# A bundle of schedule and buffer changes in a two-layer convolution and sparse-attention trunk on one core

## The chip, the core and the metric

One core of a Trainium2 chip. TensorE (PE) multiplies matrices, VectorE (DVE), ScalarE (ACT) and GpSimd (POOL) work on tiles in on-chip memory (SBUF) and, POOL excepted here, on the matrix results in PSUM; SyncE (SP) issues most DMAs. Each engine works through its own instructions in order and waits on semaphores for the others. The metric is the device time of one execution in microseconds (us).

## What is computed

Two layers over 1024 tokens of width 1024. Layer A is a gated convolution over time with a memory cross-attention beside it; layer B is a sparse attention, in which an indexer picks 256 keys a token, with its own memory attention.

```python
for i in range(DEPTH):                       # 2: layer A, layer B
    if i % N_MIXERS == 0:
        u, qm, gate = split_cols(x @ a_w_in[j], A_SIZES)
        y_mix = conformer_conv(u, ...)       # a*sigmoid(g), 31 taps a channel (1536 channels), LayerNorm, SiLU
    else:
        q, k, v, qi, ki, wi, qm, gate = split_cols(x @ b_w_in[j], B_SIZES)
        y_mix = dsa_attention(...)           # 8 index heads: sum of w*relu(qi.ki); top 256; 12 heads, one key head
    y_mem = mem_cross_attention(qm, mem_n, w_mkv)   # 4 heads into 256 memory tokens, softmax
    y = jnp.concatenate([y_mix, y_mem], axis=-1) * jax.nn.silu(gate)
    x = layer_norm(ALPHA * x + y @ w_out, pg, pb)
```

## The kernel before

Channels lie on the partitions and tokens on the free axis: a block of 128 output channels of a projection is 8 k-tiles x 3 products x 2 token halves = 48 matmuls of 128x128 by 512 columns. The three products are those of a value split in a high and a low part (`xhi`, `xlo`; weights `wh`, `wl`): high by high, low by high, high by low (L149 to L153). ACT makes a weight's high part (`wh`), POOL its low part (`wl`); activations are split from PSUM by ACT (high) and DVE (low, L169), in SBUF by ACT and POOL. Projection results stand in PSUM banks (`pj`, a ring); transposes and other small results in `pt`.

**Start and layer A.** The eight x tiles (`xn`) are transposed by `x_in` into a two-bank PSUM tile of the tag `acc` and split. `u_pair` projects a pair of channel blocks in two halves of 512 tokens, then `conv_pair` runs the 31 taps: ACT writes the scaled input to a PSUM tile `acc` (two of them), 30 taps on DVE (L429) add to it, the last one writes the SBUF tile `co`. `conv_stat` subtracts a channel mean `c_sh`, taken from the first block by a matmul with ones into an `acc` tile (`cmean`), and sums for the LayerNorm. Between the projections stand the four memory heads (`head_a`): memory tokens are transposed (`mt` to `pt` to `mf` to `mhi`, `mlo`), keys and values projected, scores, softmax (`mem_scores`: DVE maximum, ACT exponential with its sum, DVE reciprocal, POOL product by it), transposes, values. `k_b` and `v_b` do layer B's keys and values into one tile `kvr` of the tag `mp`, of which there is one buffer and which the softmax uses too. Gates are `silu_gate` (`ga`, `msgA`).

**Layer B.** Projections of gates and queries are fill, work that depends only on the layer's input. In the index stage PE makes scores `S` per index head, ACT takes the `relu`, DVE adds the weighted heads to `xs`; after each head PE issues `FILL` matmuls of gate projection. In the threshold stage DVE and ACT search the 256th largest score per token (`threshold`, `select`), while PE projects the remaining gates (`gates[FREE_GATES:]`, results through SiLU to DRAM) and the queries of the first `EARLY_Q` = 2 heads (`head_q`, high part on ACT L823, low part on DVE L824). In the attention, for each head and pair of token blocks, PE makes `S`, a DVE operation masks it and takes the maximum, ACT exponentiates, POOL divides (L975), PE transposes (`pt`), ACT and DVE split, PE multiplies by the values (`pv`). After each transposed pair `between` issues `share` steps of a fill: the query of the next head, so four blocks in three heads and one memory head; the last gate (`LATE_GATES`) is the end of it. Each query so made stays in SBUF. Output groups (L599 to L601) follow.

The order of each engine's instructions is set by a scheduler with priorities (`low`, `issue_after`) and by the tile pools, whose rings make a writer wait until the last reader is done.

## Time and profile before

| | |
|---|---|
| median of 3 runs | 1702.32 us (1701.68 to 1703.47) |
| the profiled execution | 1699.66 us |
| its span | 1697.8 us |
| PE busy | 1647.7 us, 97% |
| DVE busy | 1148.6 us, 68% |
| ACT busy | 748.3 us, 44% |
| POOL busy | 668.7 us, 39% |

Stages, in us from the span's start: layer A to about 560, its output and layer B's inputs to 860, index 860 to 914, threshold 914 to 1088, attention 1082 to about 1525, output groups to the end, with the output of the memory heads among them. A row of the time line has the start, the length, engine, line, operation and in brackets the idle time before it and what ended that.

### The profile page before, as it was taken

To read this page: it belongs to the slowest core of one execution; us is meant where nothing else is said; L and a number is where in the kernel's file an instruction comes from. 1 tells how busy PE (TensorE), PEld (TensorE's weight loads), DVE (VectorE), ACT (ScalarE), POOL (GpSimd) and SP (SyncE) were. 2 spreads that over 40 slices of the span, in tenths; PEclk is the share of its full clock that TensorE was granted. 3 is DMA by queue.
4 is the path that set the end of the run, shared out by engine and by line. 5 is a ranking of instruction groups with operands and counts; after the bars stand their busy time and mean duration, and the time that the engine had idled before them with its cause. 6 is when DMAs were issued, how large, how long until landed. Compare 5 with 4: busy or idle time off the path is not lost.

```text
span 1697.8 us, 22413 instructions
## 1 busy us (share of the span) xinstructions
PE 1647.7 (97%) x8214; PEld 1380.4 (81%) x8214; DVE 1148.6 (68%) x1798; ACT 748.3 (44%) x1395; POOL 668.7 (39%) x577
## 2 busy tenths in 40 slices
PE   8999999999989999999989999899999999999997
PEld 6877888888878788888867877688888889888886
DVE  3799999989997565256168999765455555535337
ACT  4333344444343542124466776154454544533221
POOL 2344554635556366234322332133232323332233
PEclk9999999999999999999999999899999999999999
DMA  5121212222234553122311323212122121246212
GB/s 190 46 58 66 87 51 87 63 75 63 87 124 148 206 167 131 47 79 103 84 44 51 97 83 99 82 50 69 51 75 63 61 64 50 69 163 235 87 44 99
DMA packets 137789, 152.69 MB, mean 90 GB/s; under 512 B 7946, under 2 KB 108298, under 8 KB 137680
## 3 DMA queue, kind: packets, MB, share of 16 engines
q1 hardware_dynamic: 137680, 151.27, 27.9%
q8 instruction: 64, 1.05, 0.3%
q14 instruction: 45, 0.37, 0.1%
HBM read 112.71 MB, written 36.70 MB: 88 GB/s over the span
## 4 chain that ended last, share of the span: by engine, by line
PE 52%; DVE 12%; ACT 3%; issue 2%; DMA 1%; POOL 1%; DVEq 0%; ACTq 0%; SPq 0%; POOLq 0%
PE pj L149 7%; PE pj L151 7%; PE pj L153 7%; PE pj L601 5%; PE pj L600 5%; PE pj L599 5%; DVE junk L846 4%; PE pt L995 2%; DVE xs L805 2%; PE pt L600 2%; PE pt L599 2%; PE pt L601 2%; PE S L965 1%; PE S L967 1%; PE S L966 1%
## 5 line engine op out<-in xcount | busy, mean ns | idle before, releaser
L149 PE MATMUL pj<-xhi,wh 128*128 128x512 f32 (+2 forms) x1328 | 523.4, 394 | 13.8 <-DVE ql L824 7.2
L153 PE MATMUL pj<-xhi,wl 128*128 128x512 f32 (+2 forms) x1328 | 521.6, 393 | 0.0
L151 PE MATMUL pj<-xlo,wh 128*128 128x512 f32 (+2 forms) x1328 | 520.7, 392 | 0.2 <-DVE xlo L169 0.2
L132 POOL TENSOR_TENSOR wl<-wr,wh 128x512 fp32r<-128x512 f32 x258 | 340.4, 1326 | 437.9 <-ACT wh L131 420.1
L429 DVE SCALAR_TENSOR_TENSOR acc<-h,chan,acc 128x996 f32<-128x996 f32 (+27 forms) x348 | 418.5, 1263 | 16.1 <-ACT acc L419 14.7
L149 PEld LDWEIGHTS pj<-xhi,wh 128*128 128x128 f32 (+1 forms) x1328 | 250.7, 189 | 67.3 <-DVE ql L824 7.4
L153 PEld LDWEIGHTS pj<-xhi,wl 128*128 128x128 f32 (+1 forms) x1328 | 250.6, 189 | 49.8 <-issue 0.5
L151 PEld LDWEIGHTS pj<-xlo,wh 128*128 128x128 f32 (+1 forms) x1328 | 250.8, 189 | 48.6 <-DVE xlo L169 1.0
L131 ACT ACTIVATE wh<-wr 128x512 fp32r<-128x512 f32 (+1 forms) x230 | 143.8, 629 | 317.5 <-PE pj L151 162.7
L975 POOL TENSOR_SCALAR t<-t,smB 128x128 f32<-128x128 f32 (+3 forms) x96 | 72.0, 751 | 183.5 <-DVE smB L974 95.3
L600 PE MATMUL pj<-wl,xhi 128*128 128x512 f32 x320 | 124.1, 390 | 0.0
L599 PE MATMUL pj<-wh,xhi 128*128 128x512 f32 x320 | 123.5, 391 | 0.4 <-ACT xhi L559 0.3
L601 PE MATMUL pj<-wh,xlo 128*128 128x512 f32 x320 | 122.6, 390 | 0.0
L970 DVE CUSTOM_DVE_ANT_0 t<-S,xs 128x128 f32<-128x128 f32 (+3 forms) x96 | 70.9, 755 | 74.2 <-PE S L967 49.9
L169 DVE TENSOR_TENSOR pl<-pt,ph 128x512 fp32r<-128x512 f32 (+1 forms) x120 | 69.2, 580 | 59.4 <-ACT ph L168 58.5
L168 ACT ACTIVATE ph<-pt 128x512 fp32r<-128x512 f32 (+1 forms) x120 | 60.3, 509 | 77.5 <-PE pt L995 70.6
L973 ACT ACTIVATE t<-t,mxB 128x128 f32<-128x128 f32 (+3 forms) x96 | 74.1, 774 | 45.4 <-DVE mxB L972 45.3
L852 ACT ACTIVATE junka<-xs,cand 128x896 bf16<-128x896 f32 (+2 forms) x93 | 80.3, 864 | 29.3 <-DVE cand L877 23.0
L846 DVE TENSOR_SCALAR_CACHE_REDUCE junk<-xs,cand 128x1024 bf16<-128x1024 f32 (+2 forms) x93 | 89.9, 967 | 2.2
L599 PEld LDWEIGHTS pj<-wh,xhi 128*128 128x128 f32 x320 | 60.1, 188 | 14.0 <-ACT xhi L559 1.2
L601 PEld LDWEIGHTS pj<-wh,xlo 128*128 128x128 f32 x320 | 60.0, 188 | 13.0
L600 PEld LDWEIGHTS pj<-wl,xhi 128*128 128x128 f32 x320 | 60.1, 188 | 12.9
(296 smaller groups left out, 2792.9 us busy)
## 6 DMA issues: line engine op xcount, KB each, us to landing
wr<-in_a_w_in_dram SPq DMA_DIRECT2D x88, 256.0 KB
wr<-in_b_w_in_dram SPq DMA_DIRECT2D x76, 256.0 KB
wr<-in_a_w_out_dram SPq DMA_DIRECT2D x32, 256.0 KB
wr<-in_b_w_out_dram SPq DMA_DIRECT2D x32, 256.0 KB
yraw<-yb SPq DMA_DIRECT2D x16, 512.0 KB
gb<-gB SPq DMA_DIRECT2D x15, 512.0 KB
yb<-yB SPq DMA_DIRECT2D x12, 512.0 KB
sgB<-gb SPq DMA_DIRECT2D x11, 512.0 KB
```

What stands on the lines that cost most here:

```text
L131: nc.scalar.activation(hi, raw, AF.Copy)
L132: nc.gpsimd.tensor_tensor(lo, raw, hi.bitcast(F32), op=OP.subtract)
L149: nc.tensor.matmul(o, wh, xh, start=(k == 0), stop=False)
L151: nc.tensor.matmul(o, wh, xl, start=False, stop=False)
L153: nc.tensor.matmul(o, wl, xh, start=False, stop=(k == KD - 1))
L429: nc.vector.scalar_tensor_tensor(dst[:, s:], h[:, :T - s], w, acc[:, s:], op0=OP.mult, op1=OP.add)
L599: nc.tensor.matmul(o, yh[:, k, tsl], wh, start=(k == 0), stop=False)
L600: nc.tensor.matmul(o, yh[:, k, tsl], wl, start=False, stop=False)
L601: nc.tensor.matmul(o, yl[:, k, tsl], wh, start=False, stop=(k == 3))
L846: nc.vector.tensor_scalar(j[:, :nk(b)], xs(b), th[:, i:i + 1], None, op0=op, op1=OP.add, accum_out=c[:, i:i + 1])
L852: nc.scalar.activation(j[:, :nk(b)], xs(b), AF.Sign, bias=th[:, i:i + 1], scale=-(2.0 ** 24), accum_out=c[:, i:i + 1])
L973: nc.scalar.activation(t, t, AF.Exp, bias=mx[:, e:e + 1], scale=s, accum_out=sm[:, e:e + 1])
```

## The change

1. **Start.** `wake` transposes the identity nine times before x is there. Tiles 2, 3 and 6 are transposed by halves in single banks; tiles 4 to 7 behind the first half projection and not ahead of the second; the rows of the layer's parameters are loaded and transposed at the second pair.
2. **Taps.** ACT writes the scaled input to `co` in SBUF. The first tap (s = 1) reads it and writes `acc`, the last (s = 2) writes `co`; column 1 is finished by an operation of one column.
3. **Mean.** The two halves of `cmean` go to two `pt` banks; a copy to `sumd` goes.
4. **Memory heads of layer A.** ACT multiplies by the reciprocal; the tag `mp` has two buffers, layer B's keys one of their own (`kr`), and are stored apart from the values.
5. **Layer B.** Two gates are fill in the index stage, two matmuls per head. Two late gates. Three queries (`SPILL`) are projected in the threshold stage and stored to DRAM as they are, the others and the late gates in the attention as one stream; each is fetched again by a DMA, split by ACT and POOL. The early queries' low part is made by POOL from a copy by ACT. The fill per transposed pair stays at 4 (memory heads 8).

```diff
-AHEAD = 1
-SHARE = (4, 8, 4)
-FREE_GATES = 1
+SHARE = (4, 8)
+FREE_GATES = 2
+SPILL = 3
-FILL = {7: 1, 6: 1, 5: 1, 4: 1, 3: 1, 2: 1}
-LATE_GATES = (11,)
+FILL = {7: 2, 6: 2, 5: 2, 4: 2, 3: 2, 2: 2}
+LATE_GATES = (10, 11)
...
+        def transpose_halves(src, t, bank):
+            for g in range(2):
+                o = bank()
+                for k in range(4):
+                    c = slice((4 * g + k) * P, (4 * g + k + 1) * P)
+                    nc.tensor.transpose(o[:, k * P:(k + 1) * P], src[:, c], ident)
+                split_ps(xhi[:, 4 * g:4 * g + 4, t * P:(t + 1) * P], xlo[:, 4 * g:4 * g + 4, t * P:(t + 1) * P],
+                         o.rearrange("p (a b) -> p a b", a=4))
...
+                if tags["p"][2] == 2:
+                    nc.scalar.activation(pn[:, i, :], pn[:, i, :], AF.Copy, scale=sm[:, i:i + 1])
+                else:
+                    nc.gpsimd.tensor_scalar(pn[:, i, :], pn[:, i, :], sm[:, i:i + 1], 1.0, op0=OP.mult, op1=OP.mult)
...
-                if start and hf == 1:
+                og = psum()
+                project(pg, xhi, xlo, hf * 512, 512, og)
+                if start and hf == 0:
                     for t in range(4, NB):
                         x_in(t)
+                if i == 1 and hf == 0:
                     rows_in()
-                og = psum()
-                project(pg, xhi, xlo, hf * 512, 512, og)
...
+            pair = (i0, i0 + 1)
+            accs = [psb.tile([P, T], F32, tag="acc", bufs=2, name=f"acc{i}") for i in pair]
+            for i, h in zip(pair, hs):
+                conv_out[i] = co_tile(f"co{i}")
+                nc.scalar.activation(conv_out[i], h, AF.Identity, bias=chan[:, i, TAPS:TAPS + 1],
+                                     scale=chan[:, i, TAPS - 1:TAPS])
+
+            for s in (1, *range(TAPS - 1, 1, -1)):
+                for i, h, acc in zip(pair, hs, accs):
                     w = chan[:, i, TAPS - 1 - s:TAPS - s]
+                    src, dst = (conv_out[i] if s == 1 else acc), (conv_out[i] if s == 2 else acc)
+                    nc.vector.scalar_tensor_tensor(dst[:, s:], h[:, :T - s], w, src[:, s:], op0=OP.mult, op1=OP.add)
+                    if s == 1:
+                        nc.vector.scalar_tensor_tensor(src[:, 1:2], h[:, 0:1], w, src[:, 1:2], op0=OP.mult, op1=OP.add)
...
-                o = psb.tile([P, T], F32, tag="acc", bufs=2, name="cmean")
                 for hf in range(2):
                     hs = slice(hf * 512, (hf + 1) * 512)
-                    nc.tensor.matmul(o[:, hs], ones, d[:, hs], start=True, stop=True)
-                    nc.scalar.activation(c_sh[:, hs], o[:, hs], AF.Copy, scale=1.0 / P)
+                    o = psum_t()
+                    nc.tensor.matmul(o, ones, d[:, hs], start=True, stop=True)
+                    nc.scalar.activation(c_sh[:, hs], o, AF.Copy, scale=1.0 / P)
...
+            raw = am.tile([P, NMEM], F32, tag="kr", bufs=1, name=f"kr{h}")
+            mem_k(b_w_mkv, h, raw=raw)
+            nc.sync.dma_start(kvb_dram[h][:, :NMEM], raw)
...
+                if early:
+                    raw = bq.tile([P, 512], F32, tag="qr", bufs=1, name=f"qr{h}_{hf}")
+                    nc.scalar.activation(raw, o, AF.Copy, scale=c)
+                    nc.gpsimd.tensor_tensor(ql[:, hs], raw, qh[:, hs].bitcast(F32), op=OP.subtract)
+                    continue
...
+        def raw_steps(c0, dst, pc, scale=1.0):
+            for hf in range(2):
+                o = psum()
+                yield from project_steps(pc, xhi, xlo, hf * 512, 512, o)
+                raw = bq.tile([P, 512], F32, tag="qr", bufs=1, name=f"qr{uid()}")
+                nc.scalar.activation(raw, o, AF.Copy, scale=scale)
+                nc.sync.dma_start(dst[:, hf * 512:(hf + 1) * 512], raw)
...
+        def fetch(h):
+            qh = bq.tile([P, T], F32R, tag="qh", bufs=2, name=f"qh{h}")
+            ql = bq.tile([P, T], F32R, tag="ql", bufs=2, name=f"ql{h}")
+            raw = ql.bitcast(F32)
+            nc.sync.dma_start(raw, q_d[h])
+            nc.scalar.activation(qh, raw, AF.Copy)
+            nc.gpsimd.tensor_tensor(ql, raw, qh.bitcast(F32), op=OP.subtract)
...
+            for h in line[EARLY_Q:EARLY_Q + SPILL]:
+                run(spill(h, POOL_W))
             for h in range(EARLY_Q):
-                run(head_q(h, load_cols(b_w_in, h * P)))
+                run(head_q(h, load_cols(b_w_in, h * P), True))
...
+                todo = [spill(h) for h in line[EARLY_Q + SPILL:]] + [late_gate(i) for i in LATE_GATES]
```

The new order at three places. PE at the channel mean before, `pj` 1059 being the second half of the first gate, `mt` the memory tokens:

```order
L153 MATMUL pj_1059<-xhi,wl_1030 128x512
L440 MATMUL cmean<-co_583,ones 128x512
L285 MATMUL pt_1010<-ident,mt_954 128x128
L285 MATMUL pt_1010<-ident,mt_967 128x128
L285 MATMUL pt_1000<-ident,mt_954 128x128
L285 MATMUL pt_1000<-ident,mt_967 128x128
L440 MATMUL cmean<-co_583,ones 128x512
L285 MATMUL pt_1010<-ident,mt_954 128x128
L285 MATMUL pt_1010<-ident,mt_967 128x128
L149 MATMUL pj_1111<-xhi,wh_1089 128x512
```

PE there after, followed by fourteen more transposes of `mt` and then by `pj` 1130:

```order
L153 MATMUL pj_1078<-xhi,wl_1049 128x512
L464 MATMUL pt_608<-co_542,ones 128x512
L464 MATMUL pt_611<-co_542,ones 128x512
L304 MATMUL pt_999<-ident,mt_973 128x128
L304 MATMUL pt_999<-ident,mt_986 128x128
```

ACT there after, up to the SiLU that frees the two banks of the first gate:

```order
L305 ACTIVATE mf_1010<-pt_1009,chan 128x256
L172 ACTIVATE mhi<-mf_1000 128x512
L172 ACTIVATE mhi<-mf_1010 128x512
L468 ACTIVATE sumsq<-co_542 128x1024
L305 ACTIVATE mf_1020<-pt_1019,chan 128x256 x2
L305 ACTIVATE mf_1030<-pt_1029,chan 128x256
L172 ACTIVATE mhi<-mf_1020 128x512
L340 ACT_TABLE_LOAD
L340 ACTIVATE ga_1039<-pj_1052 128x512
L340 ACTIVATE ga_1039<-pj_1078 128x512
```

The transposes of the memory tokens, which stood between projections, now stand together behind the mean.

PE in the index stage before (`S`: scores of one index head, `pj`: the gate that is fill):

```order
L149 MATMUL pj_6913<-xhi,wh_6902 128x512
L794 MATMUL S_6918<-khh,qs_6656 128x512
L795 MATMUL S_6918<-kll,qs_6656 128x512
L794 MATMUL S_6918<-khh,qs_6656 128x512
L795 MATMUL S_6918<-kll,qs_6656 128x512
L151 MATMUL pj_6913<-xlo,wh_6902 128x512
```

and after:

```order
L149 MATMUL pj_6940<-xhi,wh_6929 128x512
L151 MATMUL pj_6940<-xlo,wh_6929 128x512
L818 MATMUL S_6946<-khh,qs_6683 128x512
L819 MATMUL S_6946<-kll,qs_6683 128x512
L818 MATMUL S_6946<-khh,qs_6683 128x512
L819 MATMUL S_6946<-kll,qs_6683 128x512
L153 MATMUL pj_6940<-xhi,wl_6930 128x512
L149 MATMUL pj_6940<-xhi,wh_6929 128x512
```

Two matmuls of fill stand where one stood.

DVE at the end of the selection before (`ql`: low parts of the first query; `t`: the first masked scores):

```order
L824 SCALAR_TENSOR_TENSOR ql_8988<-pj_8989,qh_8987 128x512
L917 SCALAR_TENSOR_TENSOR eq_8033<-cs_8034,room_8038,eq_8033 128x896
L919 SCALAR_TENSOR_TENSOR xs_6309<-eq_8033,xs_6309 128x896
L824 SCALAR_TENSOR_TENSOR ql_8988<-pj_9016,qh_8987 128x512
L970 ISA t_0_9144,mxB_0_9138<-S_9140,xs_6307 128x128
```

and after:

```order
L977 SCALAR_TENSOR_TENSOR room_8145<-less_8139,cs_8141 128x1
L978 SCALAR_TENSOR_TENSOR eq_8140<-cs_8141,room_8145,eq_8140 128x896
L980 SCALAR_TENSOR_TENSOR xs_6336<-eq_8140,xs_6336 128x896
L1033 ISA t_0_9345,mxB_0_9339<-S_9341,xs_6334 128x128
```

The low parts of the queries are no longer between the selection and the first scores.

## Rows read from the trace of the kernel before

**Rows 1.** The page, part 1: engine, busy us, share of the span, instructions.

```profile
PE 1647.7 (97%) x8214; PEld 1380.4 (81%) x8214; DVE 1148.6 (68%) x1798; ACT 748.3 (44%) x1395; POOL 668.7 (39%) x577
```

**Rows 2.** Waits of PE, whole span: us in total, times, longest us.

```profile
PE pj L149 <- DVE ql L824: 7.2, 1, 7.2
PE S L794 <- ACT relu L800: 5.9, 7, 1.7
PE pj L149 <- ACT ga L321: 4.7, 2, 3.4
...
PE pj L149 <- ACT kvr L298: 1.3, 1, 1.3
```

**Rows 3.** Windows: stretch, its us, PE busy (count), other engines; an output group.

```profile
1524.00:1628.00 104.00, 104.00 (x459) 86.02 (x459) 43.37 (x54) 27.64 (x36) 32.88 (x23) 1.00 0.44 157
```

**Rows 4.** Time line of PE, between the first two half projections.

```profile
29.63 0.93 PE L263 MATMUL pj<-ident,rows 36*128 36x36 f32 x12
31.09 1.09 PE L242 MATMUL px<-ident,xn 128*128 128x128 f32 x8 [0.53 <-DVE xlo L169]
33.30 1.04 PE L149 MATMUL pj<-xhi,wh 128*128 128x512 f32 x2 [1.11 <-ACT xhi L168]
```

**Rows 5.** Time line of PE at the channel mean.

```profile
123.65 1.02 PE L440 MATMUL cmean<-co,ones 128*128 128x512 f32 x2
124.52 0.94 PE L285 MATMUL pt<-ident,mt 128*128 128x128 f32 x4
125.51 1.12 PE L440 MATMUL cmean<-co,ones 128*128 128x512 f32 x2
129.04 0.66 PE L285 MATMUL pt<-ident,mt 128*128 128x128 f32 x2 [2.41 <-ACT co L428]
131.01 0.79 PE L149 MATMUL pj<-xhi,wh 128*128 128x512 f32 x1 [1.31 <-ACT ga L321]
...
136.14 0.40 PE L149 MATMUL pj<-xhi,wh 128*128 128x512 f32 x1
```

**Rows 6.** Time line of ACT in the same stretch.

```profile
121.78 0.57 ACT L286 ACTIVATE mf<-pt,chan 128x256 f32<-128x256 f32 x1 [0.50 <-PE pt L285]
122.37 0.63 ACT L172 ACTIVATE mhi<-mf 128x512 fp32r<-128x512 f32 x1
...
129.07 1.28 ACT L321 ACT_TABLE_LOAD   x1
```

**Rows 7.** Time lines of ACT and DVE in layer A's fourth memory head.

```profile
489.17 0.20 ACT L355 ACTIVATION_READ_ACCUMULATOR mp<-pt,mx 128x1 f32 x1
...
497.54 0.39 ACT L298 ACTIVATE kvr<-pj 128x256 f32<-128x256 f32 x1
...
490.79 0.17 DVE L357 RECIPROCAL sm<-sm 128x4 f32<-128x4 f32 x1
```

**Rows 8.** The index stage: window row, and a row of DVE's time line.

```profile
860.00:914.00 54.00, 47.75 (x204) 33.59 (x203) 44.00 (x48) 39.09 (x53) 8.52 (x11) 1.00 0.09 23
...
868.47 6.83 DVE L805 SCALAR_TENSOR_TENSOR xs<-relu,win,xs 128x1024 f32<-128x1024 f32 x5
```

**Rows 9.** Time lines of PE and DVE where the attention begins.

```profile
1089.19 0.80 PE L149 MATMUL pj<-xhi,wh 128*128 128x512 f32 x1 [7.20 <-DVE ql L824]
...
1088.45 0.68 DVE L824 SCALAR_TENSOR_TENSOR ql<-pj,qh 128x512 fp32r<-128x512 f32 x1
...
1090.23 1.09 DVE L919 SCALAR_TENSOR_TENSOR xs<-eq,xs 128x896 f32<-128x896 f32 x1
```

**Rows 10.** Window of three heads and a memory head; groups of ACT and POOL.

```profile
1212.00:1316.00 104.00, 102.97 (x629) 91.90 (x628) 55.16 (x156) 52.11 (x127) 33.23 (x41) 1.00 0.21 63
...
L559 ACT ACTIVATE xhi<-yraw 128x1024 fp32r<-128x1024 f32 x14 | 14.8, 1059 | 46.8 <-DMA yraw<-yb 25.6 <-PE pj L600 20.6 <-PE pj L153 0.6
...
L560 POOL TENSOR_TENSOR xlo<-yraw,xhi 128x1024 fp32r<-128x1024 f32 x4 | 9.6, 2405 | 13.2 <-ACT xhi L559 13.2
```

**Rows 11.** Groups of POOL, 60 to 540 us and 860 to 914 us: busy, mean ns.

```profile
L132 POOL TENSOR_TENSOR wl<-wr,wh 128x512 fp32r<-128x512 f32 x103 | 133.2, 1298 | 160.9 <-ACT wh L131 149.1 <-ACT co L428 8.4 <-DMA wr<-in_a_w_mkv_dram 1.6
...
L132 POOL TENSOR_TENSOR wl<-wr,wh 128x512 fp32r<-128x512 f32 x3 | 4.7, 1595 | 0.1
```

More of the change, by code (lines that the diff above doesn't have):

```diff
@@ L499, in u_conv @@
                 conv_pair(hs, i)
+        wake()
         for t in range(4):
@@ L812, in trunk, with head_q @@
         queries = {}
-        def head_q(h, pc):
+        def head_q(h, pc, early=False):
             c = SCALE / SLOPES[h]
@@ L823, in head_q, with spill @@
                 nc.scalar.activation(qh[:, hs], o, AF.Copy, scale=c)
[L824 removed]
+                if early:
[3 more added lines that the diff above has]
+                    continue
+                nc.vector.scalar_tensor_tensor(ql[:, hs], o, c, qh[:, hs].bitcast(F32), op0=OP.mult, op1=OP.subtract)
+            queries[h] = (qh, ql)
+        line = [q for h in range(ATT_HEADS) for q in ((h, ATT_HEADS + h // 3) if h % 3 == 1 else (h,))]
+        q_d = {h: dram(f"qd{h}") for h in line[EARLY_Q:]}
+        def raw_steps(c0, dst, pc, scale=1.0):
[5 more added lines that the diff above has]
+                nc.sync.dma_start(dst[:, hf * 512:(hf + 1) * 512], raw)
+        def spill(h, pool_only=False):
+            c0 = h * P if h < ATT_HEADS else B_QM + (h - ATT_HEADS) * P
+            pc = load_cols(b_w_in, c0, pool_only=pool_only)
+            yield
+            yield from raw_steps(c0, q_d[h], pc, SCALE / SLOPES[h] if h < ATT_HEADS else 1.0)
+        def fetch(h):
[5 more added lines that the diff above has]
+            nc.gpsimd.tensor_tensor(ql, raw, qh.bitcast(F32), op=OP.subtract)
             queries[h] = (qh, ql)
@@ L1058, in trunk, with late_gate, stream @@
                                 [(partial(mem_s, m, hf), partial(mem_v2, m, hf)) for hf in range(2)]))
-            def mem_query(m, pc):
-                queries[ATT_HEADS + m] = yield from mem_q(bq, TB, pc)
-            def late_gate(i, pc):
-                g = ba.tile([P, T], F32, tag="sg", bufs=2, name=f"graw{i}")
-                for hf in range(2):
-                    o = psum()
-                    yield from project_steps(pc, xhi, xlo, hf * 512, 512, o)
-                    nc.scalar.activation(g[:, hf * 512:(hf + 1) * 512], o, AF.Copy)
-                nc.sync.dma_start(gate_d[i], g)
-            def filler(i):
-                if i + 1 < EARLY_Q:
-                    return None
-                if i + 1 < len(seq):
-                    h = seq[i + 1][0]
-                    if h < ATT_HEADS:
-                        return partial(head_q, h, load_cols(b_w_in, h * P))
-                    return partial(mem_query, h - ATT_HEADS, load_cols(b_w_in, B_QM + (h - ATT_HEADS) * P))
-                if i + 1 == len(seq) and LATE_GATES:
-                    return partial(late_gate, LATE_GATES[0], load_cols(b_w_in, B_GATE + LATE_GATES[0] * P))
-            fill, share = iter(()), 0
+            def late_gate(i):
+                pc = load_cols(b_w_in, B_GATE + i * P)
+                yield
+                yield from raw_steps(B_GATE + i * P, gate_d[i], pc)
+            def stream():
+                todo = [spill(h) for h in line[EARLY_Q + SPILL:]] + [late_gate(i) for i in LATE_GATES]
+                for k, steps in enumerate(todo):
+                    if k == 0:
+                        next(steps)
+                    if k + 1 < len(todo):
+                        next(todo[k + 1])
+                    yield from steps
+            fill, share = stream(), 0
             def between(ins):
@@ L1088, in between @@
                         next(fill, None)
-            ahead = {i: filler(i) for i in range(AHEAD)}
+            next(fill)
             seq[0][1]()
@@ L1096, in trunk @@
             for i, (h, _, units) in enumerate(seq):
-                fill = ahead[i]() if ahead[i] else iter(())
-                share = SHARE[2 if i + 1 == len(seq) else h >= ATT_HEADS]
-                ahead[i + AHEAD] = filler(i + AHEAD)
+                share = SHARE[h >= ATT_HEADS]
+                if EARLY_Q <= i + 1 < len(seq):
+                    fetch(line[i + 1])
                 for j, (sc, va) in enumerate(units):
@@ L1105, in trunk @@
                     if j == len(units) - 1 and i + 1 < len(seq):
-                        run(fill)
                         seq[i + 1][1]()
```

47 lines of the change are left out of this document (19 added, 28 removed).

## The prediction

> **What bounds the kernel now.** I read the busy shares first. TensorE is busy for 1647.7 us of a span of 1697.8 us and no other engine comes near it [rows 1], so the kernel is bound by the matrix engine, and an edit can pay only where TensorE stands still or runs at its lower clock. The list of what TensorE waited for comes next [rows 2]: one wait of 7.2 us behind the vector engine's `ql`, 5.9 us in seven pieces behind the scalar engine's `relu`, 4.7 us behind the gates `ga`, 1.3 us behind `kvr`. In gapless work of 512-column matmuls 459 start in 104 us, one each 0.227 us [rows 3]; a record is longer than that, so neighbours overlap, short gaps hide under records, and I count lost time from starts. A half block of projection is 24 matmuls, 24 x 0.227 = 5.45 us; a block of 128 columns is 10.9 us. The number of matmuls of the projections stays the same. So each part below is a question of which gap closes and which opens.
>
> The sum is made against the profiled execution, 1699.66 us (span 1697.8 and 1.9 around it). The median of the runs, 1702.32, is 2.7 us above it, and I add that at the end.
>
> **Start (part 1).** Before, between the first half projection and the second, TensorE does the transposes of the rows and of the last tile, then waits for the split of that tile, and goes on at 33.30 us [rows 4]. After, tiles 4 to 7 are transposed behind the first half and the rows' 12 small transposes go one pair later, where they cost TensorE their 0.93 us [rows 4] in any case. The first half still waits for its last weight tile, whose load stands on SP's queue behind other loads. I estimate the second half begins some 2 us earlier: 2.1 - 0.9, **-1** (ends -3 and +1: all of the 0.53 + 1.11 us waits and the move gone, or the tiles' splits in ScalarE's queue behind the sigmoid). The nine added transposes lie in time in which TensorE waits for x. The vector engine's conv starts when it did.
>
> **Channel mean (part 3).** From 123.65 to 136.14 us TensorE is 12.49 us under way [rows 5]. Work in it: 1.02 + 0.94 + 1.12 + 0.66 = 3.74 us of mean and transposes and 12 projection matmuls at 0.227, 2.7 us. So 6.0 us are lost, of which some 2.4 are the lower clock after the stall (12 starts in 5.13 us against 2.7). The new order puts both mean matmuls and all 16 transposes of `mt` in one cluster, and the next projection's bank is freed by the gate's SiLU, which on ScalarE now stands behind two `c_sh`, seven `mf`, three `mhi`, the square (1024 wide, some 1.1 us by two `mf`) and a table load of 1.28 us. With 0.57 us for an `mf`, 0.63 for an `mhi` and as much for a `c_sh` of the same shape [rows 6] that is 1.2 + 3.7 (neighbours overlap a little) + 1.9 + 1.1 + 1.3 + 0.6 (the SiLU itself, as a `c_sh`) = 9.8 us, and some 1.6 us until the first bank is full and POOL's `mlo` frees `mf`: 11.4 us, under which only 3.8 us of TensorE work lies. Lost: 7.6 + 2.4 = 10 us against 6.0: **+4** (ends -1, if the transposes really issue between projections as before, and +6). This is an edit that I expect to hurt where it stands.
>
> **Conv taps (part 2).** Two 1024-wide copies to a 1024-wide store change places, and 12 vector operations of one column (0.17 us by the four-column reciprocal of [rows 7]) are added: 2 us of DVE over 400 us in which TensorE sets the time. **0** (ends 0 and +2).
>
> **Layer A's memory heads (part 4).** In the fourth head TensorE stands 3.4 us for `ga` and 1.3 us for `kvr` [rows 2], together 4.7 us, and runs a few matmuls at the lower clock behind it. With two `mp` buffers and a separate buffer for the keys the second half of that head is spread wider and `kvr` no longer waits for it: **-5** (ends -7 and 0). Against it, ScalarE takes 32 multiplications, 0.39 us each by the copy of the same shape [rows 7], and waits in line for DVE's reciprocal: in the fourth head the last sum is there at 489.37 us and the reciprocal at 490.96, behind conv taps, 1.6 us [rows 7]. ScalarE is 44% busy [rows 1], and behind the wait stand weight splits that TensorE needs some microseconds later. I take **+1** (ends 0 and +6).
>
> **Index stage (part 5a).** From 860 to 914 us TensorE is busy 47.75 of 54 us, idle 6.25, while DVE and ScalarE are busy 44 and 39 [rows 8]; TensorE's stalls there are waits for `relu`, whose buffers DVE frees at 6.83 / 5 = 1.37 us a product [rows 8]. One block of fill is spread there now, one matmul per head; after, two matmuls per head. The second block's 10.9 us go into the gaps: the stage ends 4 to 5 us later, with 10.9 us of work less to do: **-6.5** (ends -10, the gaps hidden under records taken as well, and -2).
>
> **Threshold to attention (part 5b).** At 1089.19 - 7.20 = 1082.0 us TensorE has done its fill and four short score matmuls, and stands until 1089.19, since `ql` is queued on DVE behind the last selection, which DVE ends near 1091.3 [rows 9]; the restart costs another 2 us, by the 2.4 of the channel mean. After, TensorE has 120 more matmuls before the first scores, 27.2 us, so it comes there near 1081.5 + 27.2 - 6.5 = 1102; DVE, moved by the 4 us of the index stage, ends its selection near 1095, before that. And `ql` of the first queries comes from ScalarE and POOL, not DVE. The stall is covered twice: **-9** (ends -10 and -4).
>
> **Attention (part 5c).** 13.5 blocks of fill instead of 16 lie there, so 27 us of cover are gone. In a period of 104 us TensorE is busy 102.97, so 1 us is open now [rows 10]; ScalarE and POOL are at 52 and 33 us. Each fetched query adds one ScalarE copy of 1.06 us and one POOL subtract of 2.41 us, by the rows of these shapes [rows 10], and takes two DVE operations of 0.68 us [rows 9] away. Fill falls from some 32 to 27 matmuls per 100, so a transpose that waits for a softmax has about 1 us less work ahead of it. Four periods at up to 1 us more: **+3** (ends -3, the waits at heads' starts gone since queries are fetched early, and +12, 3 us a period).
>
> **Tail.** The second late gate is read with SiLU in the last output group, whose loads lie under the group before. **0** (ends 0 and +4).
>
> Sum: -1 + 4 + 0 - 5 + 1 - 6.5 - 9 + 3 + 0 = -13.5. 1699.66 - 13.5 = 1686.2, and with 2.7 for the median **1689 us**.
>
> One row speaks of a price in the edits that give POOL more to do. POOL's weight split of 128x512 takes 1.30 us on the mean in layer A and 1.60 us in the index stage [rows 11], where DVE multiplies and adds from two SBUF operands. The Trainium skill has the rule for it ("SBUF — State Buffer", section "Who interferes with whom"): a DVE instruction with two SBUF inputs and a GpSimd instruction that reads SBUF exclude one another, and the first to issue holds the other up. The trace agrees as far as POOL's longer time goes. In layer A it concerns the new first tap, 12 in all, off the path. Where it would change the time is rival 3.
>
> **The rivals.**
> 1. ScalarE's wait in layer A becomes TensorE's (slower). 8 half heads x (1.6 us of waiting + 4 x 0.39 us of multiplying) = 25 us more on ScalarE's queue in front of weight splits and SiLU. It decides once a wait is longer than the splits made ahead; six pairs of split buffers and 44% load speak against it, the 3.4 us wait for `ga`, which is ScalarE's lateness, for it. All of it exposed: 1689 + 24 = 1713; half, with the mean's cluster at +6: 1703 or more. Chance 0.08.
> 2. Attention gives the gain back (no change): fill thinned, queries late through DRAM, ScalarE and POOL in line behind a fetch. At +12 instead of +3, and +3 in layer A: 1701. For it: the waits for `ph` and `pt` there are many and short; against: 52% load of ScalarE. Chance 0.11.
> 3. POOL's doubled fill and early subtracts hold DVE up in the stages that DVE paces. Four more weight splits in the index stage and four subtracts before the attention, each up to 1.3 us of DVE: 5 + 5 us. The index gain falls to 1.5, and the selection ends near 1105, after TensorE arrives, so 3 us of the switch are lost: 1689 + 8 = 1697. For it POOL's 1.60 us [rows 11]; against it, there it was POOL that was late, while DVE's product of two SBUF operands kept to 1.37 us. Chance 0.07. By the page's rule in the form given above, either order can occur.
> 4. The stalls close better than I think: mean at -1, head at -7, index at -10, attention at 0: 1689 - 5 - 2 - 3.5 - 3 = 1675. Chance 0.19.
>
> **How the numbers follow.** My forecast, 1682 to 1695, has 0.55; rivals as given. Range: rival 2 and most of 4 belong in it, rival 1 not, so 1673 to 1702. What a measurement can tell from no change is 0.2%, 3.4 us: below 1698.9 is faster. Faster: 0.55 + 0.07 + 0.19 = 0.81; same: rival 2 without a tail, 0.10; slower: rival 1 and that tail, 0.09.
>
> **What would show it.** In the profile after: `ql` of the old wait gone from TensorE's list and no low clock near the switch; a `ga` wait near 130 us of 5 us or more (if it is under 3, the mean's term was wrong); the index stage nearly gapless and some 4 us longer; no wait for `kvr`; TensorE busy about 102 of each 104 us in attention. I am wrong if the periods there lengthen by over 2 us, if `mp` on ScalarE stands ahead of TensorE waits in layer A, or if DVE's products in the index stage take longer than 1.4 us.

## The result, and the profile after

The changed kernel takes 1676.32 us in the median of 4 runs (1675.28 to 1677.88), the kernel before 1702.0 in the same comparison: a ratio of 0.9854, 95% interval 0.984 to 0.9868. It is faster, by 25.7 us where 13 were forecast; the time lies in the stated range of 1673 to 1702, but 6 us below the 1682 to 1695 of the likeliest case. The profiled execution takes 1676.64 us with a span of 1674.9, 22.9 us less than before. Two executions among the runs below, one with POOL dividing (5809 us) and one with layer B's keys in `mp` (7072 us), lie far outside their like, and the medians given there leave them out.

The page's first part and the waits of PE (us in total, times, longest), to be held against [rows 1] and [rows 2]:

```profile
PE 1640.2 (98%) x8223; PEld 1377.7 (82%) x8223; DVE 1140.5 (68%) x1782; ACT 777.3 (46%) x1436; POOL 703.9 (42%) x565
```

```profile
PE pt L304 <- ACT mf L305: 3.5, 4, 2.0
PE pj L149 <- ACT ga L340: 2.9, 3, 1.7
PE pj L149 <- ACT xhi L168: 2.8, 2, 1.4
PE S L818 <- ACT relu L824: 2.6, 5, 0.8
```

The 7.2 us for `ql` and the wait for `kvr` are gone, `relu` fell from 5.9 to 2.6 us, and a wait for `mf`, the memory tokens' transposes, is new. To place the gain I compared when the n-th projection matmul starts in both traces; up to the index stage they come in nearly the same order.

| place | after minus before, us | step |
|---|---|---|
| 408th projection matmul (116 us) | -1.3 | start: -1.3 |
| 504th (152 us) | +2.5 | channel mean: +3.8 |
| 2808th (851 us, before the index stage) | -5.2 | rest of layer A: -7.7 |
| 3000th (928 us, behind it) | -13.7 | index stage: -8.5 |
| end of the span | -22.9 | threshold to the end: -9.2 |

The mean and the switch to the attention stand in the time lines of PE and DVE (answer to [rows 5] and [rows 9]):

```profile
121.86 1.88 PE L464 MATMUL pt<-co,ones 128*128 128x512 f32 x4
...
126.62 0.44 PE L304 MATMUL pt<-ident,mt 128*128 128x128 f32 x2 [0.20 <-ACT mf L305]
129.09 0.69 PE L304 MATMUL pt<-ident,mt 128*128 128x128 f32 x2 [2.03 <-ACT mf L305]
130.88 0.69 PE L304 MATMUL pt<-ident,mt 128*128 128x128 f32 x2 [1.11 <-ACT mf L305]
133.31 0.79 PE L149 MATMUL pj<-xhi,wh 128*128 128x512 f32 x1 [1.74 <-ACT ga L340]
```

```profile
1084.94 1.09 DVE L980 SCALAR_TENSOR_TENSOR xs<-eq,xs 128x896 f32<-128x896 f32 x1
1101.62 0.29 DVE L1033 CUSTOM_DVE_ANT_0 t<-S,xs 128x128 f32<-128x128 f32 x1 [15.58 <-PE S L1030]
```

From the mean to the next projection 11.45 us pass (11.4 forecast), in which the cluster of transposes waits for ScalarE's `mf` and the projection behind it 1.74 us for `ga`. At the switch the roles have turned: DVE ends its selection at 1086.0 and waits 15.58 us for TensorE's first scores. Windows of the index stage, the switch and two attention periods (stretch, its length, PE, PEld, DVE, ACT, POOL busy, granted clock, DMA; answer to [rows 8] and [rows 10]):

```profile
855.00:912.00 57.00, 54.22 (x255) 44.51 (x255) 47.50 (x49) 41.06 (x56) 12.06 (x15) 1.00 0.15 40
...
1086.00:1104.00 18.00, 17.96 (x84) 14.70 (x83) 1.52 (x9) 7.16 (x12) 10.99 (x10) 1.00 0.35 97
1104.00:1208.00 104.00, 102.75 (x630) 90.78 (x629) 55.25 (x166) 59.17 (x144) 43.65 (x49) 1.00 0.28 91
1208.00:1312.00 104.00, 102.84 (x637) 91.33 (x637) 54.14 (x159) 56.99 (x135) 43.32 (x46) 1.00 0.35 110
```

TensorE idles 2.8 us in the index stage where it idled 6.25, is gapless at the switch, and is as busy in the attention as before, though ScalarE and POOL have more to do.

### The profile page after: what moved, and what is told of

Its sections match the earlier page's. It is cut to its first block, busy times and chain, and to the rows that moved or that the text cites. A ratio compares the mean times of both kernels' runs of the same rounds, so it can differ in the third digit from the quotient of the medians.

```text
span 1674.9 us, 22548 instructions
## 1 busy us (share of the span) xinstructions
PE 1640.2 (98%) x8223; PEld 1377.7 (82%) x8223; DVE 1140.5 (68%) x1782; ACT 777.3 (46%) x1436; POOL 703.9 (42%) x565
## 4 chain that ended last, share of the span: by engine, by line
PE 76%; DVE 13%; ACT 4%; issue 2%; DMA 1%; POOL 1%; DVEq 0%; SPq 0%; ACTq 0%; POOLq 0%
PE pj L149 14%; PE pj L151 14%; PE pj L153 14%; PE pj L623 5%; PE pj L624 5%; PE pj L625 5%; DVE acc L451 4%; DVE junk L907 3%; PE pt L1058 3%; ACT junka L913 2%; PE pt L623 1%; PE S L1028 1%; PE pt L624 1%; PE pt L625 1%; PE S L1029 1%
## 5 line engine op out<-in xcount | busy, mean ns | idle before, releaser
L132 POOL TENSOR_TENSOR wl<-wr,wh 128x512 fp32r<-128x512 f32 x258 | 347.6, 1354 | 437.5 <-ACT wh L131 404.9
L451 DVE SCALAR_TENSOR_TENSOR acc<-h,chan,acc 128x1004 f32<-128x1004 f32 (+26 forms) x336 | 403.4, 1264 | 0.6
L1038 POOL TENSOR_SCALAR t<-t,smB 128x128 f32<-128x128 f32 (+4 forms) x96 | 72.0, 752 | 127.1 <-DVE smB L1037 81.2
L1033 DVE CUSTOM_DVE_ANT_0 t<-S,xs 128x128 f32<-128x128 f32 (+4 forms) x96 | 71.5, 755 | 46.1 <-PE S L1030 34.4
L1036 ACT ACTIVATE t<-t,mxB 128x128 f32<-128x128 f32 (+4 forms) x96 | 74.3, 775 | 37.7 <-DVE mxB L1035 37.0
```

What stands on the lines that cost most here:

```text
L132: nc.gpsimd.tensor_tensor(lo, raw, hi.bitcast(F32), op=OP.subtract)
L451: nc.vector.scalar_tensor_tensor(dst[:, s:], h[:, :T - s], w, src[:, s:], op0=OP.mult, op1=OP.add)
L1036: nc.scalar.activation(t, t, AF.Exp, bias=mx[:, e:e + 1], scale=s, accum_out=sm[:, e:e + 1])
```

## The experiments

Spans are compared with 1674.9 (the changed kernel) and 1697.8 (the kernel before). The first weight tiles land up to 2 us earlier or later from run to run, which moves a whole span; where it matters I take the difference from a matmul behind the start. A span is that of one execution, and four executions of one kernel lie 1 to 5 us apart, so a difference of spans under some 3 us shows nothing by itself. What TensorE "loses" in a stretch is counted from the starts of its matmuls, in gaps over 0.1 us: it holds idle time and the lower clock alike.

**The parts of layer B alone.** Parts 1 to 4 are left as before the change.

> The kernel before with part 5 (layer B) alone. Theory: the parts close separate gaps and add up. By the two traces layer B is worth -17.7 us (from 5.2 us ahead at the index stage to 22.9 at the end), so the span is 1679 to 1681 us against 1697.8 of the kernel before. By the recorded forecast for these terms (-6.5 - 9 + 3) it would be 1685. Rival: part of the gain comes from layer A's stores and buffers (separate stores of keys and values, an earlier start of the stage); then it is 1685 or more.

Measured: 1685.01 us, ratio 0.9907 (0.9893 to 0.9922), span 1683.0. At the 2808th matmul the run is 2.8 us behind the kernel before, most of it from its start, and at the end 14.8 ahead: layer B is worth -17.6 us, as the traces had it (-17.7), and does so with layer A as it was. The forecast had -12.5 for it. Layer A's parts are then worth 8.1 us by the two spans and 5.2 by the table; the 3 us between are the start.

**One gate in the index stage.**

```diff
-FREE_GATES = 2
+FREE_GATES = 1
-FILL = {7: 2, 6: 2, 5: 2, 4: 2, 3: 2, 2: 2}
+FILL = {7: 1, 6: 1, 5: 1, 4: 1, 3: 1, 2: 1}
```

> The changed kernel with one gate of fill in the index stage, one matmul per head, as before; the other gate goes to the threshold stage. Theory (the gaps of the index stage take up 48 more matmuls): TensorE loses 8.6 us there again, the first scores come 8 to 9 us later and the span is 1682 to 1684. By the recorded forecast's term it would be 1681. Rival: the threshold stage and the switch have room for that gate (DVE ends its selection 9.5 us before the first scores), and the span is 1675 to 1678.

Measured: 1683.96 us, 0.9887 (0.9872 to 0.9901), span 1681.4. It is 2.2 us ahead of the changed kernel before the index stage and 6.5 behind at the end: 8.7 us. The waits for `relu` are back at 5.6 us, and the 54 us of the stage look as before:

```profile
855.00:909.00 54.00, 47.96 (x205) 33.67 (x204) 45.51 (x48) 38.14 (x52) 7.86 (x10) 1.00 0.08 21
```

The gaps take up 48 matmuls, and the rival (room further on) falls.

**Low parts of the first queries on DVE again.**

```diff
-                run(head_q(h, load_cols(b_w_in, h * P), True))
+                run(head_q(h, load_cols(b_w_in, h * P)))
```

> The changed kernel with the low part of the first two queries made by DVE from PSUM, as before. Theory (the switch is covered by the blocks that stand ahead of it): DVE ends its selection near 1086 us, before TensorE has these queries, so `ql` no longer waits and the span is 1674 to 1677. Rival (DVE is what held the switch up, and taking `ql` from it is the cure): TensorE waits 3 us or more for `ql` near 1095 us again, span 1678 to 1683.

Measured: 1676.13 us, 0.985 (0.9828 to 0.9873), span 1674.0, and TensorE waits for nothing from 1060 to 1110 us. The switch is cured by the blocks that stand ahead of it; taking `ql` from DVE adds nothing here. Whether it would have been enough without the blocks was not run.

**Five queries ahead, not three** (`SPILL = 5`).

> The changed kernel with five queries, not three, projected in the threshold stage: two more blocks, 21.8 us of matmuls, go out of the attention. The recorded forecast gave the thinner fill there +3 us (-3 to +12) for 27 us of fill taken away. Theory by the trace (TensorE lost 13.8 us in the attention against 12.3 before, so the cover is ample): the span is 1674 to 1677. Rival (cover matters, the forecast's mechanism): the attention's losses grow by 2 to 10 us, the span is 1677 to 1685, with waits for `ph`, `pl` or `mxB`.

Measured: 1696.27 us, 0.996 (0.9945 to 0.9976), span 1693.9: 19 us lost, more than either theory said. The loss does not spread over the attention. Up to 1450 us the stretches lose what they lost in the changed kernel (the switch, with 2 us, apart); from 1450 to 1500 TensorE loses 19.7 us against 2.9. The stream of fill ends at 1450 us, 58 us before the last product with the values (in the changed kernel at 1482, 8 us before it):

```profile
1440.00:1480.00 40.00, 33.08 (x212) 28.74 (x212) 22.55 (x62) 25.16 (x61) 22.92 (x23) 0.95 0.32 106
1480.00:1510.00 30.00, 25.32 (x142) 21.83 (x141) 15.59 (x39) 12.90 (x29) 7.32 (x7) 0.84 0.10 36
```

Idle time and the lower clock come together there. So cover is not ample at all: at four matmuls per transposed pair, three queries ahead are enough for the stage and five are not. Four were not run, nor a smaller share per pair that would stretch the same fill to the end.

**Without part 4.** POOL divides, one `mp` buffer, keys and values in one tile.

> The changed kernel without part 4: POOL divides layer A's probabilities, one `mp` buffer, keys and values of layer B in one tile. Theory: the gaps that the traces show closed between 300 and 510 us (1.3 us at 343 us, 5.5 us in the fourth head) come back and the span is 1681 to 1683 us. By the recorded forecast (-5 + 1) it would be 1679. Rival: the fourth head's stall was moved by the other start and the changed mean, not by the buffers; then the span stays at 1674 to 1676.

Measured: 1696.21 us, 0.9979 (0.9968 to 0.999), span 1693.7. That is 18.8 us more than the changed kernel and even 10.7 more than layer B alone: parts 1 to 3 without part 4 make the kernel slower. The parts of layer A do not add up. Of the 18.8 us, 4.6 come at the mean, where the wait for `mf`, a tile of the same ring, grows from 3.5 to 8.8 us, and 12 between the 1500th and the 2000th projection matmul, nearly all around the fourth memory head:

```profile
PE pt L304 <- ACT mf L305: 8.8, 5, 3.3
PE pt L396 <- DVE mpl L169: 3.6, 1, 3.6
```

**POOL divides, the rest as changed.**

```diff
-                if tags["p"][2] == 2:
+                if tags["p"][2] == 3:
```

> The changed kernel with POOL, not ScalarE, multiplying layer A's probabilities; the buffers stay as changed. Recorded forecast: the multiplications on ScalarE cost 1 us (0 to 6), so the span falls to 1672 to 1675 us. Rival: POOL, which works on weight splits there, is the slower way to the probabilities, and ScalarE's multiplying is what closed part of the gaps; then the span rises to 1677 or more and TensorE waits for `mph` or `mp` between 210 and 510 us. Third way: neither, since both are covered by projections: 1674.5 to 1675.5.

Measured: 1679.08 us, 0.9876 (0.9859 to 0.9892), span 1679.1. That is 2.8 us more by the medians, 3.7 by the ratios and 4.2 by the spans: some 3 us, at the edge of what these runs can tell, where the forecast had 1 us less. TensorE does not wait for `mp` or `mph` in layer A as the rival said. DVE's conv ends 3.2 us later (546.6 against 543.4), and so does what follows. DVE's operations with two SBUF operands take 38.1 us in all, 5.6 more than in the changed kernel; why POOL's work can slow them is below.

**Keys of layer B in the `mp` ring.**

```diff
-            raw = am.tile([P, NMEM], F32, tag="kr", bufs=1, name=f"kr{h}")
+            raw = am.tile([P, NMEM], F32, tag="mp", bufs=2, name=f"kr{h}")
```

> The changed kernel with layer B's keys in a tile of the `mp` ring (two buffers) and not in one of their own. Without all of part 4 the span is 1693.7 us, with POOL dividing alone 1679.1, so some 15 us hang on the buffers. Theory: two buffers of `mp` are what matters, and the keys' own tile adds up to 2 us: span 1674 to 1677, with a wait for `kr` of under 1.5 us. Rival (the recorded forecast named both together for 5 us): the keys queue behind the softmax in the ring, TensorE stands 3 us or more in the fourth head near 490 us and the span is 1678 to 1682.

Measured: 1690.59 us, 0.9934 (0.9912 to 0.9957), span 1689.2: 14.3 us more, beyond the rival too. Between 450 and 550 us TensorE loses 16.1 us against 2.4. Its waits from 460 to 515 us:

```profile
PE pt L399 <- DVE mpl L169: 3.5, 1, 3.5
PE pj L149 <- ACT vt L325: 2.0, 1, 2.0
PE pj L149 <- ACT kr L317: 1.3, 2, 0.7
```

So with everything else of part 4 in place, the keys' small buffer decides over 14.3 us. The keys in this run share two buffers with the softmax and the values, which is not the one shared tile of the kernel before, so the 14.3 us are the price of this ring and no measure of the old one.

**Part 2 undone** (ScalarE writes the scaled input to `acc` in PSUM, 30 taps from there).

> The changed kernel with part 2 undone: ScalarE writes the scaled input to the `acc` tile in PSUM, 30 taps follow, and no vector operation of the conv reads two SBUF tiles. In the changed kernel the 12 first taps, which read `h` and `co` from SBUF, take 1.85 us on the mean and up to 2.99, and the 12 one-column operations 0.86, where a tap from PSUM takes 1.26: 17 us of DVE more than twelve taps from PSUM. Theory (DVE held by POOL in these operations): every tap is back at 1.26 to 1.28 us; against it the waits for an `acc` tile and for the copy of the first column come back, 21 us in the kernel before, of which the 10.4 us of the mean's tile stay away. So DVE's conv ends at 535 to 543 us (543.4 with the change) and the span is 1671 to 1675. Rival (the waits weigh more, as the recorded forecast's silence on them has it not): the conv ends at 547 or later and the span is 1677 to 1681.

Measured: 1676.75 us, 0.9845 (0.9829 to 0.9862), span 1674.7; the conv ends at 544.5. The same time, but by other means. Taps of the changed kernel, then of this run (count, minimum, median, maximum in ns):

```profile
L451 DVE SCALAR_TENSOR_TENSOR acc<-h,chan,acc x336: 1206/1265/1289, 56.9 to 540.8; 128x1004 f32<-128x1004 f32 x12, 128x994 f32<-128x994 f32 x7, 128x996 f32<-128x996 f32 x7, 128x998 f32<-128x998 f32 x7
L451 DVE SCALAR_TENSOR_TENSOR acc<-h,chan,co x12: 1289/1624/2989, 53.1 to 480.3; 128x1023 f32<-128x1023 f32 x12
...
L453 DVE SCALAR_TENSOR_TENSOR co<-h,chan,co x12: 204/878/2430, 56.8 to 483.3; 128x1 f32<-128x1 f32 x12
```

```profile
L453 DVE SCALAR_TENSOR_TENSOR acc<-h,chan,acc x348: 1205/1266/1289, 51.5 to 540.7; 128x1004 f32<-128x1004 f32 x12, 128x994 f32<-128x994 f32 x7, 128x996 f32<-128x996 f32 x7, 128x998 f32<-128x998 f32 x7
```

In the changed kernel the 12 first taps take 22.2 us and the 12 one-column operations 10.4; twelve taps from PSUM take 15.1. Here DVE pays for these 17.5 us with waits for ScalarE, 10.3 us in the conv alone (`acc` 2.9, `co` 7.4; 1.7 in the changed kernel). From the first tap to the last (stretch, its length, PE, PEld, DVE busy and so on; changed kernel, then this run) DVE is idle for 9.8 and for 26.2 us, and the whole is nearly as long:

```profile
53.09:543.40 490.31, 483.34 (x2374) 406.42 (x2373) 480.55 (x462) 221.10 (x383) 248.32 (x162) 0.99 0.27 82
51.50:544.50 493.00, 485.29 (x2384) 408.20 (x2383) 466.83 (x450) 227.04 (x400) 242.86 (x163) 0.99 0.27 83
```

How a one-column operation takes 2.43 us is seen where DVE and POOL are laid side by side (changed kernel, DVE, then POOL):

```profile
445.03 2.99 DVE L451 SCALAR_TENSOR_TENSOR acc<-h,chan,co 128x1023 f32<-128x1023 f32 x1
447.93 1.26 DVE L451 SCALAR_TENSOR_TENSOR acc<-h,chan,acc 128x1012 f32<-128x1012 f32 x1
449.11 2.43 DVE L453 SCALAR_TENSOR_TENSOR co<-h,chan,co 128x1 f32<-128x1 f32 x1
```

```profile
444.53 2.40 POOL L466 TENSOR_TENSOR co<-co,c_sh 128x1024 f32<-128x1024 f32 x1
446.89 2.27 POOL L132 TENSOR_TENSOR wl<-wr,wh 128x512 fp32r<-128x512 f32 x1
449.13 2.40 POOL L472 TENSOR_TENSOR sumd<-sumd,co 128x1024 f32<-128x1024 f32 x1
```

The first tap begins inside POOL's subtraction and ends 1.1 us after it; the weight split that POOL began meanwhile takes 2.27 us and not 1.30 ([rows 11]); the one column takes as long as POOL's addition beside it. The tap from PSUM between them keeps its 1.26 us. The Trainium skill ("SBUF — State Buffer", section "Who interferes with whom") says that a DVE instruction with two SBUF inputs and a GpSimd instruction that reads SBUF exclude one another; the trace agrees, in both directions. The trace shows one more case: an operation on a single SBUF operand of two columns, the scaling of the softmax's maximum, is held as well. It takes 0.16 us where POOL is idle and 2.36 beside a POOL addition, with which it ends (DVE, then POOL):

```profile
396.43 2.36 DVE L371 TENSOR_SCALAR mx<-mx 128x2 f32<-128x2 f32 x1
```

```profile
395.50 3.26 POOL L472 TENSOR_TENSOR sumd<-sumd,co 128x1024 f32<-128x1024 f32 x1
```

**DVE scales the input itself.**

```diff
-                nc.scalar.activation(conv_out[i], h, AF.Identity, bias=chan[:, i, TAPS:TAPS + 1],
-                                     scale=chan[:, i, TAPS - 1:TAPS])
+                nc.vector.tensor_scalar(acc, h, chan[:, i, TAPS - 1:TAPS], chan[:, i, TAPS:TAPS + 1], op0=OP.mult, op1=OP.add)
```

with the last tap and the copy of the first column as in the kernel before.

> The changed kernel with another part 2: DVE makes the scaled input itself, from `h` in SBUF into the `acc` tile in PSUM, so neither ScalarE's copy nor a first tap with two SBUF operands is there; the last tap and the copy of the first column are as before the change. Theory: 12 operations of 1.1 to 1.3 us take the place of 17 us of delay, DVE does not wait for ScalarE, and the conv ends 2 to 8 us earlier than 543.4; the end of layer A follows the conv (`tot` starts 12 to 14 us after it in five runs), so the span is 1668 to 1674. Rival: layer A's end is set by TensorE's own work, and the span stays at 1674 to 1676 whatever the conv does.

Measured: 1688.63 us, 0.9914 (0.9899 to 0.9929), span 1685.7. The operations take 1.34 us each, but the conv ends at 559.4, 16 us later, not earlier. From the first tap to the last DVE takes 508.9 us, 18.6 more than in the changed kernel, and the trace says where they lie: 12.3 more are idle (DVE waits 6.7 us for `co`, 5.6 for `kva` and 5.6 for `sm`), and 6.5 are the sixteen two-column scalings, which take 12.0 us and not 5.5, since more of them fall beside POOL's work; the conv's own operations take 0.8 less. The theory of this run counted neither. Why the waits grew stays open. What the run also shows is that layer A's end follows the conv. TensorE keeps its pace to 550 us and then waits for DVE's sums and splits:

```profile
PE pt L621 <- DVE accA L626: 4.8, 2, 2.7
PE pt L623 <- DVE ylo L582: 4.3, 2, 3.6
```

**The mean back in an `acc` tile.**

> The changed kernel with one edit undone: the channel mean goes to an `acc` tile again, as before. In the changed kernel's trace TensorE is put back by 3.8 us between the 408th and the 504th projection matmul (from 1.3 us ahead of the kernel before to 2.5 us behind). Theory: the two `pt` banks of the mean are the cause, since the transposes of the memory tokens must wait for them and so stand together behind the mean. Then the transposes go between the projections again, TensorE is 3 to 6 us earlier from 150 us on, and the span is 1669 to 1672 us (1674.9 with all of the change). Rival: the two `mp` buffers or the new start make the cluster; then the stall stays and the span is 1674 to 1676. Second rival: the vector engine waits for an `acc` tile as before, its conv ends later than the end of layer A allows, and what TensorE gains at 130 us it waits for near 550 us: span 1674 to 1676 with a new wait there.

Measured: 1680.22 us, 0.9883 (0.9868 to 0.9898), span 1681.3. TensorE idles 1.5 us between 118 and 138 us where it idles 5.7 in the changed kernel, and is 8.5 us ahead of it at the 504th matmul, more than the theory said. Yet the kernel is slower, by 3.9 us in the median and 6.4 in the profiled execution, which is the slowest of the four. DVE waits 3.9 us for the tile and its conv ends at 553.5, 10 us later; TensorE loses 8.2 us between 300 and 350 us (0.2 in the changed kernel) and 5.9 from 600 to 860 (2.9 there), waiting for `ga`, `kva`, `mp` and `accA`. The second rival holds, and by more than the gain.

**Memory tokens earlier.** Their preparation stands ahead of the first conv, so that their transposes do not queue behind the mean; the mean keeps its two banks.

```diff
-        u_conv(0)
-        u_conv(2)
-        mem_prep()
+        hs0 = [u_pair(0, start=True), u_pair(1)]
+        mem_prep()
+        with low(50000):
+            conv_pair(hs0, 0)
+        u_conv(2)
```

> The changed kernel with the memory tokens' preparation written ahead of the first conv and not behind the second pair: its transposes lie between the projections at 70 to 95 us, and nothing stands in the ring of `pt` banks behind the channel mean. Theory (TensorE and DVE bound layer A together): the mean's 9.6 us stall goes nearly whole, so TensorE is 7 to 9 us ahead of the changed kernel at the 504th projection matmul; but DVE's conv still ends near 543 us, and the runs so far put the end of layer A 12 to 14 us behind it, with some 4 us of slack at the output group's wait for `accA`. So 4 to 5 us are kept and the rest comes back as TensorE's waits between 250 and 640 us: span 1669 to 1672. Rival (TensorE alone sets the time, as the recorded forecast argued): all of it is kept, span 1665 to 1668.

Measured: 1676.02 us, 0.9854 (0.9824 to 0.9884), span 1674.9. The stretch from 118 to 138 us is gapless; in the changed kernel it is idle for 5.7 us and at a granted clock of 0.76 (this run, then the changed kernel):

```profile
118.00:138.00 20.00, 20.00 (x90) 16.57 (x89) 20.00 (x19) 6.20 (x9) 3.88 (x3) 1.00 0.17 53
```

```profile
118.00:138.00 20.00, 14.26 (x49) 9.26 (x48) 20.00 (x19) 13.25 (x21) 9.96 (x7) 0.76 0.22 79
```

TensorE is 12.1 us ahead at the 504th matmul and 0.7 us at the 2520th. The rest was given back, for the most part in waits for DVE and ScalarE (the longest of 250 to 860 us):

```profile
PE pt L625 <- DVE accA L630: 2.7, 1, 2.7
PE pj L149 <- DVE kva L169: 2.1, 2, 1.9
PE pj L149 <- ACT ga L340: 1.8, 2, 1.5
```

The theory held DVE's conv to end near 543 us, but here it ends at 549.1, 5.7 us later, and 3.5 us of that are again the two-column scalings, which more often meet POOL's work (9.0 us and not 5.5). So the run shows that this way of closing the stall gains nothing. It does not show that the stall itself was free: an edit that closes it and leaves DVE where it was has not been run.

**The same, and the one-column operation on ScalarE.**

```diff
-                    if s == 1:
-                        nc.vector.scalar_tensor_tensor(src[:, 1:2], h[:, 0:1], w, src[:, 1:2], op0=OP.mult, op1=OP.add)
+                nc.scalar.activation(conv_out[i][:, 1:2], h[:, 0:1], AF.Identity, bias=conv_out[i][:, 1:2],
+                                     scale=chan[:, i, TAPS - 2:TAPS - 1])
```

> As the run with the early memory tokens, and the one-column operation of each conv block goes from DVE to ScalarE, where it stands right behind the scaled input. In the changed kernel these 12 take 10.3 us of DVE, 0.86 each, since POOL holds the port that a second SBUF operand needs. Theory: DVE's conv ends 6 to 10 us earlier than without this edit (near 535 us), so layer A's end no longer waits for it and the span is 1664 to 1668, 3 to 5 us less than with the early tokens alone. Rival: DVE has slack there; then this run and the one with early tokens alone are within 1 us.

Measured: 1674.94 us, 0.9842 (0.9817 to 0.9866), span 1672.5. DVE's conv takes 9.4 us less, but ends 2.5 us earlier (546.6 against 549.1), and the span falls by those 2.4 us. DVE waits more in between (`sm` 7.8 us, 2.3 in the run above). It is the best median of all, 1.1 us below the run above, but its interval holds the ratios of both that run and the changed kernel, so no gain is shown.

In the four runs in which TensorE came early or DVE late (the mean in `acc`, DVE scaling, both with early memory tokens) the index stage starts 295.8 to 297.7 us after the conv's last tap. In the changed kernel it starts 302.1 after it. I read this as DVE's chain standing only some 5 us behind TensorE's in layer A: a gain of TensorE there beyond that is not kept unless DVE gains too.

## Why the prediction was right, and where its sizes were off

The time lies in the stated range and moved the forecast way, but it came in 5.7 us below the likeliest case, and the reading that the sum stands on holds for the average only.

- **What bounds the kernel:** the prediction took TensorE alone, since no other engine comes near its 97% of the span. In layer A another does. DVE is busy for 92 to 98 of each 100 us there from 100 to 500 us, as this window of the kernel before shows (DVE is the third figure):

```profile
200.00:300.00 100.00, 99.77 (x488) 83.92 (x488) 97.66 (x97) 47.07 (x85) 55.38 (x44) 1.00 0.22 69
```

- **Start:** -1 forecast, -1.3 read. In the ten runs with the new start and the old place of the tokens the 408th matmul comes 0.8 to 2.9 us before that of the kernel before, in the run with layer B alone 1.7 after it, so the sign is shown and the size is not.
- **Channel mean:** +4 forecast, +3.8 read, by the named mechanism: memory tokens behind the mean in the `pt` ring, SiLU behind them on ScalarE. But the prediction's own sign fails: it said that the term is wrong if the wait for `ga` is under 3 us, and that wait is 1.74. The time lies in the waits for `mf` ahead of it (2.03 and 1.11 us). What the step did not see is DVE: closing the stall by early memory tokens left the time as it was, and the old place of the mean, which the step held to be the better one, costs 3.9 us in the median.
- **Conv taps:** 0 forecast, and undoing them changes the span by 0.2 us. But the working was wrong. The one-column operations take 0.86 us on the mean, not 0.17, and the first taps 1.85, not 1.26; the edit adds 17.5 us to DVE and saves about as much in waits (9.8 us idle and not 26.2). That the two cancel was luck. "Off the path" was wrong for the first tap too: the end of layer A follows DVE's conv. The rule on the shared port stood in the prediction with the right operations beside it, and I weighed it only for layer B (rival 3).
- **Layer A's heads:** -5 + 1 = -4 forecast, -7.7 read. The direction and the two stalls named were right: neither returns. The size was off, and the sign of the second term was: ScalarE's multiplication is a gain of some 3 us, with 5.6 us less in DVE's two-operand operations, and not a cost of 1. Rival 1 (ScalarE's wait becomes TensorE's) shows nowhere.
- **Index stage:** -6.5 forecast, -8.5 read, 8.7 by the run with one gate. I took the idle 6.25 us of the window as nearly all there was; the gaps hidden under overlapping records, which I put at the far end only, belong in the term. The stage is 2 us longer, not 4 to 5. Rival 3 does show, though small: DVE's 1024-wide products take 1.28 us on the mean before and after, but all 48 products take 47.4 us, 1.7 more than before, with four weight splits of POOL among them and not three (beside one a 384-wide product takes 1.47 us, alone 0.62). TensorE's gain came in all the same. The prediction's argument against it, that DVE's product "kept to 1.37 us", was read from 1024-wide products that stood alone: in the same stage of the kernel before, a 640-wide one beside a weight split took 1.72 us.
- **Switch:** -9 forecast. From 1050 to 1100 us TensorE lost 10.2 us and now none. Of the two covers the blocks alone are enough, as the run with `ql` on DVE shows.
- **Attention:** +3 forecast. From 1100 to 1500 us the loss goes from 12.3 to 13.8 us, +1.5; the kernel before is in its attention until 1512 us and loses another 1 there, so the stage as a whole costs 0 to 1.5. The mechanism, thinner fill that exposes a little everywhere, is not what the run with five queries shows: fill per pair stays at four, and what is missing is missing at the end, all at once. With five queries ahead it cost 19 us. That the fill of the changed kernel ends 8 us before the last product, and not 58, was luck of my term, not its reasoning.
- **The median:** I added 2.7 us, the distance of the median from the profiled run before. After, the two agree within 0.3 us, so about 3 us of the miss are this offset, which a single profiled run cannot give.

The sum of the terms was -13.5 and the spans differ by 22.9. Of the 9.4 us between, 3.7 are layer A's heads, 2 the index stage, 3.2 the switch with the attention and what follows. The time fell where rival 4 was put (1675), but only in part by its way: the head term came to its value (-7.7 for -7), the index and attention terms lie about midway between the forecast's and its, the mean term stayed at the forecast's, and the 3 us of the offset fill the place.

## What to carry to other kernels

Where one engine is 97% busy, look stage by stage for the second that is nearly as full: here 12 us of TensorE's time gained at 130 us bought nothing, as DVE's conv ended later. Count fill against the places that take it, so that it reaches the end of the stage that needs it: where it ended 58 us early, TensorE lost 19.7 us in 50. A small buffer of its own for a value that shares a ring with a slow user can be worth more than moving work between engines (14.3 us against some 3).

## What the runs showed of the hardware

A DVE operation on one column with two SBUF operands took 2.43 us beside a POOL addition of 2.40, and 0.20 to 0.22 where POOL was idle; a tap with two SBUF operands took up to 2.99 us (3.32 with POOL dividing) and 1.29 where POOL was idle. A scaling of two columns with one SBUF operand took 0.16 and up to 2.36 us. Taps with one operand in PSUM stayed between 1.21 and 1.29 us in all 336. So in these rows it is not the width of such an operation that sets its time, but how long the POOL operation beside it still has to go. With idle gaps of 1.1 to 2.0 us at the mean TensorE's granted clock over 118 to 138 us was 0.76, with the matmuls behind them starting 0.43 us apart at first, the lower of its two levels (1.2 and 2.4 GHz); in the same stretch without the gaps it was 1.00.
